# A fixed pipelined order for the last eight value projections, with the loads and the inversion at the delta rule's end rearranged

## The chip, the cores and the metric

The kernel runs on one core of a Trainium2 chip. The metric is the time of one execution on the device in microseconds (us). Five engines work side by side, each through its own instructions in order: PE (matmul), DVE (vector), ACT (scalar, also a DMA issuer), POOL (GpSimd) and SP (here only a DMA issuer). An instruction waits on semaphores for data of other engines and of DMA transfers; everything behind it on its engine waits too.

## The reference

One inference step of a two-layer encoder over 2048 prompt tokens and 32 sample tokens, 1024 wide, all in float32. Layer 1 is a gated delta rule of eight heads of 128, layer 2 is windowed attention. Cut to what the change touches:

```python
def causal_conv(x, buf, w):                      # four taps, then SiLU
    xp = jnp.concatenate([buf, x], axis=1)
    y = sum(xp[:, j:j + l] * w[j] for j in range(4))
    return jax.nn.silu(y), xp[:, -3:]

def delta_layer(x, conv_buf, s0, w_in, ...):
    proj = x @ w_in                              # q | k | v | z | a | b
    qkv, new_buf = causal_conv(proj[..., :3072], conv_buf, conv_w)
    q, k = l2norm(qkv[..., :1024]) * 128 ** -0.5, l2norm(qkv[..., 1024:2048])
    g, beta = -exp(a_log) * softplus(a + dt_bias), sigmoid(b)
    # blocks of positions: decay = exp(gcum_i - gcum_j); (I + lower) is inverted;
    # S = S * exp(gcum_last) + kdec^T v_new along the blocks
    o, s_new = gated_delta_rule(q, k, v, g, beta, s0)
    o = o * rsqrt(mean(o * o) + eps) * norm_w * silu(z)
    return layer_norm(ALPHA * x + o @ w_out, ln_g, ln_b), new_buf, s_new
```

The second layer projects queries and gates from the result, attends over the last two blocks of 64 and its own, and ends in a second output projection and layer norm.

## The kernel before

Every wide projection is split into three float32r products: weights and activations are each parted into a high part (a cast on ACT) and a low part (a subtraction on DVE or POOL), and `project` adds hi·hi, hi·lo and lo·hi in PSUM.

**Projection rows.** In `P1.qkv`, row i (0 to 23) is 128 columns of w_in: 0 to 7 are q heads, 8 to 15 k heads, 16 to 23 v heads. A row is five blocks of 416 tokens; a block is 24 matmuls (L77 to L79) into one of six PSUM banks, and ACT copies it to the row tile R (L258, two buffers). Weights come by SP into `w_raw` (L46, one buffer), ACT casts `w_hi` (L53), POOL subtracts `w_lo` (L54), two buffers each. Then the row's convolution: ACT writes the first tap (L198), DVE adds three more (L200, three instructions), ACT takes tanh (L203), DVE finishes SiLU (L204), SP stores 1 MB to `s_v` (L206; `s_k`, `s_q` for the other kinds). After each eighth row of q and k, `norms` runs a chain of small DVE operations on [128, 136].

**Work laid beside rows 16 to 23.** `decays` makes 34 decay matrices: a load of `gcum` into E (L231, ACT's queue, three buffers), an addition on DVE (L239), four exponentials on ACT (L243), a store to `s_E` (L244, ACT's queue). `split_out_weights` takes one piece of the output weights per row from row 7 on: fetch by SP (L1037) into the tile that tanh also uses, cast on ACT (L1038), subtraction on POOL (L1039), store `s_wo` by SP (L1040). In all of this the framework's scheduler sets each engine's order.

**Gate rows and the delta rule.** Rows 24 to 31 (`P1.z`) are the gate, of which three blocks each come ahead of the delta rule. `Delta.run` then walks 17 chunks (one of the sample, 16 of the prompt) through steps named in the table `ORDER`, which with a planner fixes PE, DVE and ACT; loads (`load`, L598 to L611) go by SP. Each chunk inverts a triangular matrix: the first `SPLIT` of 31 column steps on POOL (`early`, L661 and L663), the rest on DVE (`late`). In the last chunks a second generator, `O1.tiles`, the output projection with its norm (matmuls L1075 to L1077), is given out in small pieces as filler by `second.give`. Output weights come back by ACT's queue, slice by slice, at the calls of `side`; the tiles g (L1105), r (L1110) and the norm's tables (L1058, L1059) by SP. `first_end` finishes the sample chunk (transposes `otr<-ident,os` L848, gate L852). At the very end the last chunk's o is normalised (`OSC`, whose last step is L839) and transposed.

**Layer 2** begins by splitting the activations of its five blocks (L68, L69) under the first matmuls of `P2.gate`.

Of the kernel before, what the change touches and what calls it, by code (L numbers as in the profile page):

```python
# [18 lines left out]

D = 1024  # L20
NP = 2048
# [74 lines left out]
class P1:  # L96

    def __init__(self, tc, left, right, mid, I, O, T, G):  # L100
        self.nc, self.I, self.O, self.T, self.G = tc.nc, I, O, T, G
# [44 lines left out]
    def qkv(self):  # L146
# [31 lines left out]
        matrices = self.decays()  # L178
        wo = split_out_weights(nc, one, "th", I["a_w_out"], T["wo"])
        for i in range(24):  # L180
            kind, h = i // 8, i % 8
# [7 lines left out]
            if 7 <= i < 23:  # L189
                next(wo)  # L190
            if i >= 16:
                for _ in range(5 if i < 18 else 4):
                    next(matrices)
            nc.gpsimd.tensor_copy(self.convo[:, i, 0:3], R[:, NP:NP + 3])  # L194
            nc.gpsimd.tensor_copy(self.convo[:, i, 3:6], R[:, NT + 3:NT + 6])
            W = NT + 3
            y = big.tile([128, NT + 3], F32, tag="y", name="y")
            nc.scalar.activation(y[:], R[:, 0:W], AF.Copy, scale=self.convw[:, i, 0:1])  # L198
            for j in range(1, 4):
                nc.vector.scalar_tensor_tensor(out=y[:], in0=R[:, j:j + W], scalar=self.convw[:, i, j:j + 1], in1=y[:],  # L200
                                               op0=ALU.mult, op1=ALU.add)
            th = one.tile([128, NT + 3], F32, tag="th", name="th")
            nc.scalar.activation(th[:], y[:], AF.Tanh, scale=0.5)  # L203
            nc.vector.scalar_tensor_tensor(out=y[:], in0=th[:], scalar=1.0, in1=y[:], op0=ALU.add, op1=ALU.mult)  # L204
            dst = T["qkv"[kind]]
            nc.sync.dma_start(dst[0:NTT - 1, :, h, :].rearrange("t p k -> p t k"),  # L206
                              y[:, 0:NP].rearrange("p (t k) -> p t k", k=128))
            nc.scalar.dma_start(dst[NTT - 1, :, h, 0:NS], y[:, NP + 3:NP + 3 + NS])
            if kind == 2:
                continue  # L210
            nc.scalar.activation(th[:, 0:NP], y[:, 0:NP], AF.Square)
            nc.scalar.activation(th[:, NP:NT], y[:, NP + 3:NP + 3 + NS], AF.Square)
            nc.vector.transpose(R[:, 0:NT], th[:, 0:NT])
            nc.vector.tensor_reduce(out=parts[:, h, :], in_=R[:, 0:NT].rearrange("p (c j) -> p c j", j=32),
                                    axis=AX.X, op=ALU.add)
            if h == 7:
                norms(nc, G, parts, self.sel, kind, one, self.pt)
        nc.sync.dma_start(self.O["conv"][:, :, :], self.convo[:])

    def decays(self):  # L220
# [6 lines left out]
        def load(m):  # L227
# [3 lines left out]
            nc.scalar.dma_start(E[:, :, :n], T["gcum"][t, hs, :n].partition_broadcast(128))  # L231
            return E, t, n, hs

        ahead = load(0)
        for m in range(len(todo)):
# [8 lines left out]
            nc.scalar.dma_start(T["E"][t, :n, hs, :n], E[:n, :, :n])  # L244
# [15 lines left out]
    def z(self, blocks, pool, tags, ps, sub, w):  # L260

        nc = self.nc
        for h in range(8):
            self.fetched = fetch_weights(nc, self.wp, self.I["w_in"][25 + h]) if h < 7 else None
            self.next, self.sub = None, sub
            for b in blocks:
                p = ps()
                yield from project(nc, p[:, :TB], w, self.x[b])
                th = pool.tile([128, TB], F32, tag=tags[0], name="zth")
# [267 lines left out]
class Delta:  # L537
# [6 lines left out]
    SPLIT = 25  # L544
# [121 lines left out]
    def early(self, ch, j):  # L666
        cut = [self.SPLIT * i // 6 for i in range(7)]
        drain(self.chain(ch, self.nc.gpsimd, cut[j], cut[j + 1], "tm" if j == 0 else None))

    def late(self, ch, j):  # L670
        cut = [self.SPLIT + (31 - self.SPLIT) * i // 3 for i in range(4)]
# [231 lines left out]
    def run(self, chunks, S, gate, second, side, done):  # L903
# [4 lines left out]
        for c, ch in enumerate(chunks):  # L908
            ch.S, ch.last = (self.S if ch.pool is None else S), ch.pool is not None or c == last
        gate.plan(order, self.FIRST + 2, self.WHOLE)  # L910
        gate.begin()
        for i in range(self.FIRST, last + 4):
# [3 lines left out]
            for p, (name, off) in enumerate(order):  # L916
# [4 lines left out]
                elif 0 <= c <= last and self.wanted(chunks[c], name):  # L921
# [3 lines left out]
                    if c == last and name == "oa1":  # L925
# [3 lines left out]
                if i >= self.OPEN and p % (len(order) // 5) == 10:  # L929
# [4 lines left out]
    def first_end(self, c0, second, done):  # L934
        second.give(2.0)
# [3 lines left out]
        second.give(3.0)  # L939
# [4 lines left out]
        done(c0)  # L944

# [109 lines left out]
def ln_tables(nc, pool, g, b):  # L1055
    gt = pool.tile([128, D], F32, tag="ln_g", name="ln_g")
    bt = pool.tile([128, D], F32, tag="ln_b", name="ln_b")
    nc.sync.dma_start(gt[:], g.partition_broadcast(128))  # L1058
    nc.sync.dma_start(bt[:], b.partition_broadcast(128))  # L1059
# [30 lines left out]
class OutNorm:  # L1090


    def __init__(self, tc, es, name, side, I, pre, banks, kept):
# [4 lines left out]
        self.tabs = None  # L1098
        self.tables = lambda: ln_tables(nc, self.one, I[pre + "_ln_g"], I[pre + "_ln_b"])
# [3 lines left out]
    def fetch(self, src, n):  # L1103
        g = self.one.tile([128, KC, 128], F32, tag="g", name="g")
        self.nc.sync.dma_start(g[:, :, :n], src)  # L1105
# [52 lines left out]
class O1:  # L1158
# [13 lines left out]
    def turned(self, h, c0, row, n):  # L1172
# [3 lines left out]
        for q in range(2):  # L1176
# [4 lines left out]
            copy = nc.scalar.copy if q == 0 or c0 == 0 else nc.vector.tensor_copy  # L1181
# [5 lines left out]
    def tiles(self, tiles, ready, more):  # L1187
# [8 lines left out]
        for i, t in enumerate(tiles):  # L1196
# [5 lines left out]
            following = self.rows(*tiles[i + 1]) if i + 1 < len(tiles) else None  # L1202
            for j, out in enumerate(self.on.tile(got, r, t[2], True)):
# [15 lines left out]
class P2:  # L1219
# [26 lines left out]
    def load(self, b, res):  # L1246
# [8 lines left out]
        self.x[b] = split_acts(nc, res, b, raws, nc.gpsimd if b < 2 else nc.vector)  # L1255
# [105 lines left out]
class Attention:  # L1361
# [27 lines left out]
    def open_right(self, right):  # L1389
# [9 lines left out]
        self.tabs = ln_tables(self.nc, self.oone, I["b_ln_g"], I["b_ln_b"])  # L1399
# [444 lines left out]
```

## Time and profile before

| what | value |
|---|---|
| median of 3 runs | 2211.59 us (2209.03 to 2213.85) |
| profiled execution | 2210.17 us, its span 2208.4 us |
| PE busy | 2151.5 us, 97% of the span |
| DVE, ACT, POOL busy | 1373.8, 900.9, 825.7 us |
| mean granted clock of PE | 0.991 |
| DMA | 308.29 MB, 140 GB/s on average |

A busy row of PE counts matmuls whose ends are modelled. The views by stretch give busy time in each stretch and the granted clock of PE in it; the waits of PE name what ended each idle time. Value rows 16 to 23 run from about 398 to 589 us, the gate rows follow; the end of the delta rule lies from 1000 to 1170, layer 2 begins behind it.

### The profile page before, as it was taken

What the parts mean: (1) busy time and instruction counts of PE and PEld (TensorE: products, weight loads), DVE (VectorE), ACT (ScalarE), POOL (GpSimd) and SP (SyncE); (2) the same over time, 40 slices, a digit from 0 to 9 for tenths busy, and PEclk for the clock granted to TensorE, in tenths of its full rate; (3) what the DMA queues carried; (4) which work ended last, traced back from release to release, by engine and by line L of the source; (5) the groups of instructions that cost most, each with busy time, mean ns of one, the idle gap of its engine ahead of it and who ended that gap; (6) DMA issues with size and microseconds to landing.
All of it is one profiled execution on the core that took longest, in us unless ns stands there. A gap on an engine that the chain in (4) does not pass through costs nothing.

```text
span 2208.4 us, 36899 instructions
## 1 busy us (share of the span) xinstructions
PE 2151.5 (97%) x13690; PEld 1982.6 (90%) x13690; DVE 1373.8 (62%) x2701; ACT 900.9 (41%) x2274; POOL 825.7 (37%) x1201
## 2 busy tenths in 40 slices
PE   8999999999899999998999999999999999999998
PEld 6999999999899999998987887999999987778885
DVE  3676666664468588777867876125442236668775
ACT  4344344455522466665741212222112235544442
POOL 1422223211122377777720301046442124555564
PEclk9999999999999999999999999999999999999999
DMA  5222333356654544447735764365212287233321
GB/s 197 68 61 87 103 111 106 95 169 199 198 165 131 178 149 160 148 160 257 254 96 179 233 195 124 124 209 176 82 66 79 85 185 265 77 96 96 98 71 53
DMA packets 268116, 308.29 MB, mean 140 GB/s; under 512 B 79728, under 2 KB 198832, under 8 KB 267664
## 3 DMA queue, kind: packets, MB, share of 16 engines
q1 hardware_dynamic: 245696, 268.50, 39.1%
q10 hardware_dynamic: 22240, 37.42, 5.2%
q8 instruction: 108, 1.77, 0.3%
q14 instruction: 72, 0.59, 0.1%
HBM read 189.63 MB, written 116.60 MB: 139 GB/s over the span
## 4 chain that ended last, share of the span: by engine, by line
PE 65%; DMA 6%; DVE 3%; POOL 2%; ACT 1%; issue 1%; ACTq 0%; SPq 0%; DVEq 0%; POOLq 0%
PE ps L77 9%; PE ps L79 8%; PE ps L78 8%; PE po L1075 5%; PE po L1077 5%; PE po L1076 5%; PE ot L1567 4%; PE S L1546 2%; PE tr L1561 2%; DMA wo_parts<-in_a_w_out 1%; DMA E<-s_gcum 1%; PE g L627 1%; PE gq L754 1%; PE sp L769 1%; PE ks L769 1%; PE vp L769 1%
## 5 line engine op out<-in xcount | busy, mean ns | idle before, releaser
L77 PE MATMUL ps<-act_hi,w_hi 128*128 128x416 f32 x2000 | 708.5, 355 | 10.2 <-ACT R L258 6.1
L79 PE MATMUL ps<-act_hi,w_lo 128*128 128x416 f32 x2000 | 707.0, 354 | 3.3 <-POOL w_lo L301 1.8
L78 PE MATMUL ps<-act_lo,w_hi 128*128 128x416 f32 x2000 | 704.0, 352 | 2.5 <-DVE act_lo L69 2.5
L77 PEld LDWEIGHTS ps<-act_hi,w_hi 128*128 128x128 f32 x2000 | 377.8, 189 | 18.0 <-ACT R L258 7.1
L79 PEld LDWEIGHTS ps<-act_hi,w_lo 128*128 128x128 f32 x2000 | 377.4, 189 | 8.9 <-POOL w_lo L301 2.1
L78 PEld LDWEIGHTS ps<-act_lo,w_hi 128*128 128x128 f32 x2000 | 377.7, 189 | 8.4 <-DVE act_lo L69 3.9
L54 POOL TENSOR_TENSOR w_lo<-w_raw,w_hi 128x1024 fp32r<-128x1024 f32 x44 | 117.3, 2667 | 481.3 <-ACT w_hi L53 421.4
L200 DVE SCALAR_TENSOR_TENSOR y<-R,convw,y 128x2083 f32<-128x2083 f32 x72 | 181.8, 2526 | 41.3 <-POOL convo L194 22.5
L661 POOL TENSOR_TENSOR tm<-L,Tt 128x60 f32<-128x60 f32 (+19 forms) x375 | 130.4, 348 | 104.6 <-issue 40.2
L1554 POOL TENSOR_TENSOR P<-P,sm 128x384 f32<-128x384 f32 (+2 forms) x128 | 101.6, 816 | 169.2 <-DVE sm L1432 100.2
L663 POOL TENSOR_TENSOR Tt<-Tt,tm 128x60 f32<-128x60 f32 (+19 forms) x375 | 143.8, 384 | 29.4
L1428 ACT ACTIVATE P<-S,nm 128x192 f32<-128x192 f32 (+3 forms) x260 | 104.8, 418 | 90.5 <-DVE nm L1421 43.9
L258 ACT COPY R<-ps 128x416 f32<-128x416 f32 (+1 forms) x144 | 60.6, 444 | 131.0 <-PE ps L79 107.8
L1075 PE MATMUL po<-wo_hi,g_hi 128*128 128x512 f32 x256 | 104.3, 407 | 0.0
L1077 PE MATMUL po<-wo_hi,g_lo 128*128 128x512 f32 x256 | 100.8, 394 | 0.5 <-DVE g_lo L1118 0.5
L1076 PE MATMUL po<-wo_lo,g_hi 128*128 128x512 f32 x256 | 100.6, 393 | 0.0
L1272 POOL TENSOR_TENSOR rs<-rs,sin 128x416 f32<-128x416 f32 x50 | 70.6, 1413 | 78.1 <-DVE rs L1271 71.4
L1567 PE MATMUL ot<-pt,vd 128*128 128x256 f32 x372 | 97.9, 390 | 1.9 <-ACT pt L1563 1.4
L53 ACT CAST w_hi<-w_raw 128x1024 fp32r<-128x1024 f32 x48 | 50.4, 1049 | 112.6 <-PE ps L78 82.9
L1075 PE MATMUL po<-wo,g_hi 128*128 128x512 f32 x224 | 92.9, 415 | 0.0
L1357 DVE SCALAR_TENSOR_TENSOR za<-zs,za 128x416 f32<-128x416 f32 x40 | 33.3, 834 | 93.0 <-ACT za L1356 92.9
L1077 PE MATMUL po<-wo,g_lo 128*128 128x512 f32 x224 | 90.1, 402 | 0.0
(301 smaller groups left out, 4067.1 us busy)
## 6 DMA issues: line engine op xcount, KB each, us to landing
w_raw<-in_w_in SPq DMA_DIRECT2D x40, 512.0 KB
w_raw<-in_b_w_in SPq DMA_DIRECT2D x20, 512.0 KB
k<-s_k SPq DMA_DIRECT2D x17, 512.0 KB
E<-s_E SPq DMA_DIRECT2D x17, 512.0 KB
s_bz<-za SPq DMA_DIRECT2D x40, 208.0 KB
s_bq<-ra SPq DMA_DIRECT2D x40, 208.0 KB
s_q<-y SPq DMA_DIRECT2D x8, 1024.0 KB
s_wo<-wo_parts SPq DMA_DIRECT2D x16, 512.0 KB
```

The costliest lines, as they stand in the source:

```text
L54: sub.tensor_tensor(out=lo[:], in0=raw[:], in1=hi[:], op=ALU.subtract)
L77: nc.tensor.matmul(ps, hi[:, k, :], xh[:, k, :], start=(k == 0), stop=False)
L78: nc.tensor.matmul(ps, hi[:, k, :], xl[:, k, :], start=False, stop=False)
L79: nc.tensor.matmul(ps, lo[:, k, :], xh[:, k, :], start=False, stop=(k == KC - 1))
L200: nc.vector.scalar_tensor_tensor(out=y[:], in0=R[:, j:j + W], scalar=self.convw[:, i, j:j + 1], in1=y[:], op0=ALU.mult, op1=ALU.add)
L661: P.tensor_tensor(out=tm[:n, i0 - k:, :w], in0=L[:n, i0:, j:j + 1].to_broadcast(sh), in1=Tt[:n, j:j + 1, :w].to_broadcast(sh), op=ALU.mult)
L663: P.tensor_tensor(out=Tt[:n, i0:, :w], in0=Tt[:n, i0:, :w], in1=tm[:n, i0 - k:, :w], op=ALU.subtract)
L1075: nc.tensor.matmul(ps[:n], ghi[:, k, :n], w[0][:, k, cs], start=a, stop=False)
L1076: nc.tensor.matmul(ps[:n], ghi[:, k, :n], w[1][:, k, cs], start=False, stop=False)
L1077: nc.tensor.matmul(ps[:n], glo[:, k, :n], w[0][:, k, cs], start=False, stop=z)
L1428: nc.scalar.activation(P[u], src, AF.Exp, bias=nm[:, u:u + 1], scale=1.0, accum_out=sm[:, u:u + 1])
L1567: nc.tensor.matmul(ot[:, p], self.vd[:, kc0 + j, p, :], pt[:, 2 * j:2 * j + 2, :], start=(j == 0), stop=(j == nj - 1))
```

## The change

It has three parts. **(A)** Rows 0 to 15 stay as they were (their convolutions up to 14). For rows 16 to 23, `ordered` writes the order of PE, DVE, ACT and SP by hand: in row i, `conv` of row i − 1 is dealt out in steps between the five blocks, one decay matrix is made ahead of each block of rows 17 to 23, and one output weight piece per row follows the convolution's store. The loads and stores of E, and the short store of each row, go by SP's queue instead of ACT's. The tail of row 23's convolution is dealt out between the first 13 steps of the gate rows, which for that take two tiles of the old pool. **(B)** In the delta rule's last chunks (behind number 11, `OPEN`) `SPLIT` is 23 instead of 25; the loads of g, r and the norm's tables in that part go by ACT's queue (`self.queue`, until the first tile of the rest), the output weights in four calls of `side` per chunk instead of five; `first_end` is called behind `OSC` of the last chunk and not behind `oa1`, and gives 5.5 us of filler in one piece ahead of the sample chunk's transposes and 1.5 behind. **(C)** Gate block 0 of layer 2's second slab moves ahead into the filler's last part; block 2's activation subtraction goes from DVE to POOL; the last short tile's copies go to DVE.

```diff
-        for i in range(24):
+        for i in range(self.FREE + 1):            # FREE = 15
...
+            if i < self.FREE:
+                drain(self.conv(i, R, parts))
+        with self.tc.manual_schedule(engines={ET.PE, ET.DVE, ET.Activation, ET.SP}):
+            self.ordered(R, parts, wo)
...
+    def ordered(self, R, parts, wo):
+        nc, I = self.nc, self.I
+        w = split_weights(nc, self.wp, I["w_in"][self.FREE + 1], nc.gpsimd)
+        matrices = None
+        for i in range(self.FREE + 1, 24):
+            c = self.conv(i - 1, R, parts)
+            nxt = self.row(i)
+            raw = fetch_weights(nc, self.wp, I["w_in"][i + 1])
+            next(c)
+            for b in range(NB):
+                if matrices:
+                    next(matrices, None)
+                for _ in range((2, 2, 1, 1, 0)[b]):
+                    next(c, None)
+                if b == 3:
+                    next(wo)
+                self.block(nxt, w, b)
+                if b == 0:
+                    following = split_fetched(nc, self.wp, raw, nc.gpsimd)
+            drain(c)
+            R, w = nxt, following
+            if i == self.FREE + 1:
+                matrices = self.decays()
+                next(matrices)
+        self.room = self.one, ("parts", "gtmp")
+        self.tail = self.conv(23, R, parts)
+        next(self.tail)
+        self.w24 = w
...
-            nc.scalar.dma_start(E[:, :, :n], T["gcum"][t, hs, :n].partition_broadcast(128))
+            nc.sync.dma_start(E[:, :, :n], T["gcum"][t, hs, :n].partition_broadcast(128))
-            nc.scalar.dma_start(T["E"][t, :n, hs, :n], E[:n, :, :n])
+            nc.sync.dma_start(T["E"][t, :n, hs, :n], E[:n, :, :n])
...
+    with tc.manual_schedule(engines={ET.PE, ET.DVE}):
+        for a, b in ((2, 5), (2, 4), (1, 4)):
+            for _ in range(a):
+                next(p1.tail)
+            for _ in range(b):
+                next(z)
+        drain(p1.tail)
...
-    SPLIT = 25
+    SPLIT = 25, 23
+            ch.split = self.SPLIT[c > self.OPEN]
...
-                    if c == last and name == "oa1":
+                    if c == last and name == "OSC":
                         self.first_end(chunks[0], second, done)
-                if i >= self.OPEN and p % (len(order) // 5) == 10:
+                if i >= self.OPEN and p % (len(order) // 4) == 10:
...
     def first_end(self, c0, second, done):
-        second.give(2.0)
...
-        second.give(3.0)
+        second.give(5.5)
...
+        second.give(1.5)
...
+        self.tabs, self.queue = None, nc.scalar
-        self.nc.sync.dma_start(g[:, :, :n], src)
+        self.queue.dma_start(g[:, :, :n], src)
-        self.nc.sync.dma_start(r[:n], src)
+        self.queue.dma_start(r[:n], src)
...
-        self.x[b] = split_acts(nc, res, b, raws, nc.gpsimd if b < 2 else nc.vector)
+        self.x[b] = split_acts(nc, res, b, raws, nc.gpsimd if b < 3 else nc.vector)
...
+            if i == 2:
+                yield from p2[0].gate(1, (0,), p2[0].ps)
```

The order of SP in the value rows, one row of before (E's transfers were on ACT's queue):

```order
L206 DMA s_v<-y 128x16x128
L1037 DMA wo_parts<-in_a_w_out 128x512
L46 DMA w_raw<-in_w_in 128x1024
L1040 DMA s_wo<-wo_parts 128x2x512
L206 DMA s_v<-y 128x16x128
```

and the same place after, from the store of one row's third matrix on (L271 and L285 are E's load and store, L216 and L218 the stores of v, L1080 and L1083 the fetch and store of the output weights, L47 the next weights):

```order
L271 DMA E<-s_gcum 128x512
L285 DMA s_E<-E 128x512
L216 DMA s_v<-y 128x16x128
L218 DMA s_v<-y 128x32
L1080 DMA wo_parts<-in_a_w_out 128x512
L1083 DMA s_wo<-wo_parts 128x2x512
L271 DMA E<-s_gcum 128x512
L285 DMA s_E<-E 128x512
L47 DMA w_raw<-in_w_in 128x1024
L271 DMA E<-s_gcum 128x512
```

The first load of the next row's matrices now stands behind the store of the output weights, and the store of v behind that of a matrix.

DVE at the end of the key norms, before (L398 to L405 are the norms, L200 and L204 row 16's and 17's convolution, L239 a matrix):

```order
L239 TENSOR_TENSOR E<-E,nm 128x512
L398 SCALAR_TENSOR_TENSOR n_lt<-n_ly,n_lt 128x136
L399 TENSOR_TENSOR n_ly<-n_lt 128x136
L400 TENSOR_SCALAR n_lx<-n_ly 128x136
L402 SCALAR_TENSOR_TENSOR n_lx<-n_lx,n_ly 128x136 x6
L403 TENSOR_SCALAR n_lx<-n_lx 128x136
L200 SCALAR_TENSOR_TENSOR y<-R,convw,y 128x2083
L404 TENSOR_TENSOR n_lx<-n_lx,n_lt 128x136
L200 SCALAR_TENSOR_TENSOR y<-R,convw,y 128x2083
```

and after (L442 to L447 the norms, L207 and L213 the convolution, now of row 16, L280 a matrix):

```order
L442 TENSOR_SCALAR n_lx<-n_ly 128x136
L444 SCALAR_TENSOR_TENSOR n_lx<-n_lx,n_ly 128x136 x6
L445 TENSOR_SCALAR n_lx<-n_lx 128x136
L446 TENSOR_TENSOR n_lx<-n_lx,n_lt 128x136
L447 TENSOR_TENSOR t_ngc<-t_ngc,n_lx 128x136
L280 TENSOR_TENSOR E<-E,nm 32x4x32
L207 SCALAR_TENSOR_TENSOR y<-R,convw,y 128x2083 x2
L280 TENSOR_TENSOR E<-E,nm 32x4x32
L207 SCALAR_TENSOR_TENSOR y<-R,convw,y 128x2083
L280 TENSOR_TENSOR E<-E,nm 128x512
L213 SCALAR_TENSOR_TENSOR y<-th,y 128x2083
```

The norms are one piece now, and row 16's convolution begins behind them.

DVE at the end of the last chunk, before (otr_11916 and otr_11923 are the sample chunk's transposed o, otr_11962 the last chunk's; L817 updates the state, L839 is the end of OSC):

```order
L1083 SCALAR_TENSOR_TENSOR r<-r,po 128x512
L1135 BN_STATS st<-r 128x6
L852 TENSOR_TENSOR z<-otr_11916,z 128x4x32
L852 TENSOR_TENSOR z<-otr_11923,z 128x4x32
L817 SCALAR_TENSOR_TENSOR Sp<-Sp,t_egl,sp_11868 128x128 x4
L830 SCALAR_TENSOR_TENSOR Xo<-Xo,t_eq 128x8
```

and after, from the end of OSC (L881) on:

```order
L881 TENSOR_TENSOR o<-o,ro_y 128x1024
L1161 TENSOR_TENSOR g_lo<-g,g_hi 128x1024
L1126 SCALAR_TENSOR_TENSOR r<-r,po 128x512
L1178 BN_STATS st<-r 128x6
L894 TENSOR_TENSOR z<-otr_11960,z 128x4x32
L1126 SCALAR_TENSOR_TENSOR r<-r,po 128x512
```

The sample chunk's gate (otr_11960) stood ahead of the last chunk's state and OSC, and now stands behind them.

More of the change, by code (lines that the diff above doesn't have):

```diff
@@ L188, in qkv @@
                     self.block(R, w, b)
-            if 7 <= i < 23:
+            if 7 <= i < self.FREE:
                 next(wo)
[L191 to L205, printed above, removed]
@@ L1180, in turned @@
                 nc.tensor.transpose(tr[:, j, :n], h[:n, k * 128:k * 128 + 128], self.G["ident"][:n, :n])
-            copy = nc.scalar.copy if q == 0 or c0 == 0 else nc.vector.tensor_copy
+            copy = nc.scalar.copy if n == 128 and (q == 0 or c0 == 0) else nc.vector.tensor_copy
             copy(hT[:, q * 4:q * 4 + 4, :n], tr[:, :, :n])
@@ L1607, in program @@
     next(ahead)
-    w = p1.first_gate(nc.gpsimd)
-    z = p1.z((0, 1, 2), zp, ("zth", "z"), p1.ps, nc.gpsimd, w)
-    with tc.manual_schedule(engines={mybir.EngineType.PE, mybir.EngineType.DVE}):
-        for _ in range(28):
+    with tc.manual_schedule(engines={ET.PE, ET.DVE}):
+        for _ in range(15):
             next(z)
@@ L1661, in program @@
     o1[0].bank = p2[0].ps
-    with tc.manual_schedule(engines={ET.PE, ET.DVE}):
-        second.rest()
-    left.close()
-    p2 = p2[0]
     with tc.manual_schedule(engines={ET.PE}):
+        with tc.manual_schedule(engines={ET.DVE}):
+            second.rest()
+        left.close()
+        p2 = p2[0]
         p2.open_left(left)
-        drain(p2.gate(1, (0, 1), p2.ps))
+        drain(p2.gate(1, (1,), p2.ps))
     for b in (2, 3, 4):
```

75 lines of the change are left out of this document (49 added, 26 removed).

## The prediction

> **What bounds the kernel now.** I read the page first, then PE's waits, then busy time by stretches of 40 us, and then the rows around each wait.
>
> The page's rows of busy time, as engine, busy us, share of the span, instructions:
>
> ```profile
> span 2208.4 us, 36899 instructions
> PE 2151.5 (97%) x13690; PEld 1982.6 (90%) x13690; DVE 1373.8 (62%) x2701; ACT 900.9 (41%) x2274; POOL 825.7 (37%) x1201
> ```
>
> PE bounds it: only 2208.4 − 2151.5 = 57 us of PE's time are idle. No edit here removes a matmul from PE, so a gain is idle time taken away plus work no longer done at the low clock, and any new idle time of PE is a loss. The change reaches PE's idle time in three places. Place A is the value projections; the stretches (us, then busy time of PE, PEld, DVE, ACT, POOL, the granted clock, DMA share, GB/s) and PE's waits from 398 to 645:
>
> ```profile
> 480.00:520.00 40.00, 40.00 (x214) 39.73 (x213) 22.18 (x17) 20.64 (x48) 5.01 (x8) 1.00 0.66 199
> 520.00:560.00 40.00, 38.44 (x205) 37.84 (x203) 16.13 (x12) 20.47 (x49) 7.05 (x7) 1.00 0.66 201
> 560.00:600.00 40.00, 35.41 (x169) 34.30 (x170) 21.64 (x16) 22.69 (x52) 6.59 (x9) 0.91 0.63 203
> 600.00:640.00 40.00, 35.91 (x192) 34.31 (x191) 19.15 (x15) 15.00 (x22) 8.56 (x5) 0.96 0.61 168
> ...
> PE ps L77 <- ACT R L258: 6.1, 2, 3.2
> PE ps L77 <- ACT w_hi L309: 2.3, 1, 2.3
> PE ps L79 <- POOL w_lo L301: 1.8, 1, 1.8
> ```
>
> PE idles 6.1 + 2.3 + 1.8 = 10.2 us here, all after 556. The clock of 0.91 and 0.96 in the two stretches after idle time means about (0.09 + 0.04) × 40 = 5 us of work lost at the low clock. A perfect order is worth 15 us at place A. PE ran full until about 556 although ACT and DVE were behind, because its six PSUM banks and two weight sets let it run ahead.
>
> Place B is the end of the delta rule: stretches, PE's waits (1015 to 1170), one wait of DVE.
>
> ```profile
> 1000.00:1040.00 40.00, 37.54 (x462) 35.92 (x460) 34.75 (x92) 28.66 (x95) 32.28 (x90) 1.00 0.81 289
> 1040.00:1080.00 40.00, 34.74 (x354) 33.93 (x354) 27.61 (x68) 24.23 (x80) 25.69 (x76) 0.91 0.75 267
> 1160.00:1200.00 40.00, 35.74 (x161) 29.66 (x162) 27.93 (x78) 6.44 (x8) 2.99 (x2) 0.91 0.61 187
> ...
> PE otr L848 <- DVE o L839: 5.7, 1, 5.7
> PE g L627 <- DMA k<-s_k: 4.2, 1, 4.2
> PE y1p L697 <- DVE tcp L678: 2.6, 2, 1.6
> PE vtr L741 <- DMA v<-s_v: 2.0, 1, 2.0
> ...
> DVE tm L661 <- POOL Tt L663: 6.3, 3, 2.4
> ```
>
> Each 0.91 is 0.09 × 40 = 3.6 us lost at the low clock.
>
> **Place A, part by part.** Here the change writes one order for PE, DVE, ACT and SP. What decides is the loop from one value row to the next. From 495 to 526 before shows every link of it; the columns are start, duration, engine, line, operation, and the idle time with its releaser:
>
> ```profile
> 495.51 0.38 SPq L206 DMA_DIRECT2D s_v<-y  x1
> 500.67 2.39 POOL L54 TENSOR_TENSOR w_lo<-w_raw,w_hi 128x1024 fp32r<-128x1024 f32 x1 [11.14 <-ACT w_hi L53]
> 502.88 0.62 ACT L1038 CAST wo_parts<-wo_parts 128x512 fp32r<-128x512 f32 x1 [1.83 <-DMA wo_parts<-in_a_w_out]
> 504.16 0.33 ACTq L231 DMA_DIRECT2D E<-s_gcum  x1
> 505.35 1.26 ACT L243 ACTIVATE E<-E,t_ngc 128x128 f32<-128x128 f32 x4
> 505.50 0.38 SPq L1040 DMA_DIRECT2D s_wo<-wo_parts  x1
> 507.93 0.69 DVE L239 TENSOR_TENSOR E<-E,nm 128x512 f32<-128x512 f32 x1 [3.60 <-DMA E<-s_gcum]
> 511.44 4.80 DVE L200 SCALAR_TENSOR_TENSOR y<-R,convw,y 128x2083 f32<-128x2083 f32 x2
> 517.99 1.95 ACT L203 ACTIVATE th<-y 128x2083 f32<-128x2083 f32 x1 [3.15 <-DVE E L239]
> 521.68 2.32 DVE L204 SCALAR_TENSOR_TENSOR y<-th,y 128x2083 f32<-128x2083 f32 x1
> 524.03 0.38 SPq L206 DMA_DIRECT2D s_v<-y  x1
> ```
>
> Before, the loop takes 524.03 − 495.51 = 28.5 us. In the new order it is, link by link: s_v issued until the output weight behind it has landed, 502.88 − 495.51 = 7.4; its cast and subtraction until s_wo is issued, 505.50 − 502.88 = 2.6. Only then does SP issue the next row's first load of a decay matrix, where ACT used to issue it beside this: 0.4. From that issue to its use 507.93 − 504.16 = 3.8, and about 1.5 more since the 0.5 MB of s_wo now stand ahead in the same queue (an estimate: half of what those 7.4 us hold beside the 3.8 of a lone transfer, which is 1 MB's share). Then DVE in its fixed order: addition 0.7, three convolution steps with an addition between, 1.5 × 4.80 + 0.7 = 7.9; tanh 1.95; last step 2.3. SP next owes the store of the fourth matrix, so one more addition and four exponentials, 0.7 + 1.3 + 0.4 = 2.4, before the next s_v. Sum: 7.4 + 2.6 + 0.4 + 5.3 + 0.7 + 7.9 + 1.95 + 2.3 + 2.4 = 31 us. As the three or four gaps that ACT's own issues made there go, I take **30 us a row**, 28 to 32 for its bounds. PE needs 22.5 a row (five blocks of 24 matmuls, full in 480 to 520 with 214 in 40 us).
>
> What waits behind this on PE: the weights of row i+1 are cast on ACT only behind row i's first exponentials and first copy, so PE's start follows the loop once about a row of lead is used up. The loop also starts later: all small operations of the key norms stand on DVE ahead of the first value row's convolution, where before they lay between its steps. The rows of before: the reduction that the norms need, two of the norms' operations, and PE's first matmul of the first gate row:
>
> ```profile
> 419.58 2.32 DVE L214 TENSOR_REDUCE parts<-R 128x65 f32<-128x2080 f32 x1
> 435.52 0.30 DVE L443 SCALAR_TENSOR_TENSOR n_t<-n_x,n_y 128x136 f32<-128x136 f32 x1
> 435.86 0.30 DVE L445 TENSOR_TENSOR n_t<-n_t,n_y 128x136 f32<-128x136 f32 x1
> 589.22 0.62 PE L77 MATMUL ps<-act_hi,w_hi 128*128 128x416 f32 x1 [2.98 <-ACT R L258]
> ```
>
> 35 such operations at 435.86 − 435.52 = 0.34 are 12 us, from about 423 (419.58 + 2.32, and the norms' matmuls) to 435. Row 18's weights are then ready at 435 + 0.7 (addition) + 1.3 (exponentials) + about 1.5 (copy and cast on ACT) + 2.4 (w_lo on POOL), near 440, and those of the first gate row, number 24, six loops later at 440 + 180 = 620. Before, PE began that row at 589.2. So +31, less what before still lost behind that point (waits of 2.3 and 1.8, the 1.6 of clock 0.96 and about half of the 3.6 of 0.91: 7.5), plus 1.7 for the low clock behind a new wait of 7 us: **+25**, from +13 (28 us a row) to +37 (32). If PE stayed full all the way it would be −15. Row 23's convolution moves between the first 13 steps of the gate rows; its four large steps on DVE (about 10 us) lie beside 13 quarters of a block, 15 us of matmuls, and cost PE nothing; were they not covered, it would be one wait of about 3 us for a bank. The Trainium skill (DMA: Bandwidth & Descriptors, Issuing engines are not separate DMA queues) says that issuing on several engines saves only the sequencer's time to start a DMA; by that sentence alone, moving the matrices from ACT to SP is free, and place A would come out at its gain of 15. The trace's rows speak against free: the row of 505.50 shows SP held until the subtraction is done, and the load would now stand behind it.
>
> **Place B.** First, a burst of 2.5 MB (g, the two norm tables, two residual tiles) goes from SP to ACT's queue, about 90 us later; the loads of the output weights go from five to four per chunk.
>
> ```profile
> 1017.04 2.20 SPq L1105 DMA_DIRECT2D g<-s_g  x1
> 1036.53 0.32 SPq L598 DMA_DIRECT2D k<-s_k  x1
> ```
>
> The queues are full behind it (DMA share 0.81), k lands 8 us after its issue, and PE waits 2.0 + 4.2. That goes, and the 3.6 at the low clock: −9 (if other loads keep the queue full, −3). On ACT five issues now stand between the last chunk's copies; by the rows above one is 0.32 to 2.2 us, two or three of them on PE's path: +1.5 (0 to +4). Second, the split: two of 25 inversion steps of the last five chunks go from POOL to DVE. PE's 2.6 us for tcp hang on DVE's 6.3 us for POOL. POOL saves 2 × (0.348 + 0.384) = 1.5 us a chunk by the page's means of L661 and L663; what DVE adds I bound by the same 1.5 and by nothing:
>
> ```profile
> L661 POOL TENSOR_TENSOR tm<-L,Tt 128x60 f32<-128x60 f32 (+19 forms) x375 | 130.4, 348 | 104.6 <-issue 40.2
> L663 POOL TENSOR_TENSOR Tt<-Tt,tm 128x60 f32<-128x60 f32 (+19 forms) x375 | 143.8, 384 | 29.4
> ```
>
> Net −1.5 (0 to −2.6). Third, the sample chunk's end is placed behind the last chunk's normalised output instead of ahead of it:
>
> ```profile
> 1158.37 0.54 DVE L852 TENSOR_TENSOR z<-otr,z 128x128 f32<-128x128 f32 x2 [1.66 <-PE otr L848]
> 1164.26 1.08 PE L848 MATMUL otr<-ident,o 128*128 128x128 f32 x4 [5.68 <-DVE o L839]
> ```
>
> DVE idled 1.66 for os, and o was there only at 1164.2. Without that wait, the gate steps for os (0.54 × 2) and one residual addition with its statistics (1.4) ahead of it, o is there near 1159 to 1160. PE has six more matmuls and four transposes (about 2 us) to do before it asks for o, so from 1158.6, where it began to wait, it goes on to about 1160.6: −5.7 − 3.6 + 0.5 of DVE work moved behind, about **−8.5** (−5 to −9). Place B: −9 + 1.5 − 1.5 − 8.5 = **−17.5**, from −8 to −22.
>
> **Place C**, the start of layer 2's projection, 1360 to 1395:
>
> ```profile
> PE ps L78 <- DVE act_lo L69: 2.5, 4, 1.3
> PE ps L77 <- ACT act_hi L68: 1.8, 2, 1.0
> ```
>
> Half a pair of blocks is moved ahead as cover and block 2's subtraction goes to POOL: of 4.3 us and about 1.7 at the low clock I take −3 (−6 if all goes, +2 if POOL's 2.4 us for a subtraction, the row of 500.67, take the place of DVE's).
>
> **Sum.** +25 − 17.5 − 3 = +4.5. The profiled execution took 2210.2 (span 2208.4), so it would take 2214.7; the median of the runs lies 1.4 above it, which makes **2216**. About 0.2% (4.4 us) is what a measurement of this kernel can tell from no change, so the forecast stands at that edge, on the slow side. Its own range, with a loop of 29 to 31 us and B from −22 to −12, is 2205 to 2222.
>
> The low clock in the sum is the trace's 0.91; the Trainium skill (TensorE: Matmul & The Clock Gate, What's actually happening) gives 3.4 us at half rate behind an idle window. By that each of about five new waits of 7 us costs 1.7; I count only the last, since the earlier rows have 7 us of slack against the loop. The trace's stretch of 560 to 600 shows low clock behind waits of only 3 us.
>
> **The rivals.** (1) *PE stays full, or nearly, at A*: the loop comes out at 26 us or less because ACT no longer stops for issues and landings (the tanh row has 3.15 idle ahead of it, and ACT is busy half of the time). At 25 and below A is −15 to −5 and the kernel ends at 2211.6 − 15 − 17.5 − 3 = 2176 to 2186; at 26 A is +1 and it ends at 2192. Against it: s_v, output weight, s_wo and the next load stand in one line on SP, 7.4 + 2.6 + 0.4 + 5.3 = 16 us by themselves, and the DVE and ACT steps that follow are another 15. (2) *One queue makes the loop longer still*, and from about 30 us a row on the kernel is slower by more than 4.4: at 32 us it ends at 2211.6 + 37 − 17.5 − 3 = 2229. For it: the DMA share is 0.66 in this stage with two queues at work, and now one carries all. (3) *B does not pay*: the 2.5 MB and the output weights meet other loads later, so that −9 is −3, and ACT's five issues cost 4; B is then −9 and the kernel ends at 2211.6 + 25 − 9 − 3 = 2225. For it: the 16 output-weight loads still run beside the chunks' loads. (4) *What binds at A is something that the order doesn't touch*, and the rest is hidden: 2212 ± 3.
>
> **How the numbers follow.** Forecast: 0.35, of it 0.05 faster, 0.14 within 4.4 us and 0.16 slower. Rival 1: 0.26, all faster, half of it below 2184. Rival 2: 0.19 and rival 3: 0.15, all slower. Rival 4: 0.05, the same. Faster 0.05 + 0.26 = 0.31; same 0.14 + 0.05 = 0.19; slower 0.16 + 0.19 + 0.15 = 0.50. The range 2184 to 2234 leaves out the fuller half of rival 1 (0.13) and a loop over 33 us (0.05).
>
> **What would show it.** In the profile after: s_v stores of rows 18 to 22 spaced 28 to 32 us; PE waits of 5 to 9 us for w_hi or w_lo at the start of each of rows 20 to 24; the output-weight store followed at once on SP by a load of E, whose addition ends DVE's longest idle time. At B no wait of PE for k near 1040, none for o at the last chunk, a clock of 1.00 there. I am wrong if the s_v stores come every 23 to 26 us and PE shows no wait in 440 to 640, or if the waits at B stay with other names.

## The result: slower by 1.5%, and where the time went

The changed kernel takes 2243.5 us (median of 4 runs, 2242.5 to 2246.7) against 2210.7 of before (now also a median of 4): a ratio of 1.0149, interval 1.0132 to 1.0167, or +32.8 us. The forecast was 2216, its range ended at 2234. The direction was right, the size was not. The page of after:

```profile
span 2242.2 us, 36907 instructions
PE 2158.0 (96%) x13690; PEld 1988.5 (89%) x13690; DVE 1387.3 (62%) x2718; ACT 899.4 (40%) x2273; POOL 833.9 (37%) x1185
```

PE runs the same 13690 matmuls and is busy 6.5 us longer, at a mean granted clock of 0.985 where before had 0.991; the rest of the loss is idle time. The same matmul, found in both traces by its place among those of its kind, shows where the lag arises:

| matmul of | before, us | after, us | lag | arisen since the row above |
|---|---|---|---|---|
| first value row | 398.22 | 398.28 | 0.1 | |
| first gate row's start | 589.22 | 630.35 | 41.1 | +41.1, value rows |
| gate rows, middle | 699.97 | 750.67 | 50.7 | +9.6, behind the value rows |
| delta rule, chunk near 1020 | 1019.99 | 1070.68 | 50.7 | 0 |
| behind the loads of 1017 | 1059.96 | 1102.88 | 42.9 | −7.8, loads and split |
| output projection, 1130 | 1130.04 | 1172.15 | 42.1 | −0.8 |
| behind the sample chunk's end | 1199.99 | 1233.84 | 33.9 | −8.3, sample chunk's end |
| layer 2, behind its first blocks | 1410.04 | 1440.35 | 30.3 | −3.5, place C |
| attention | 1900.15 | 1934.03 | 33.9 | +3.6 |

Places B and C gave −16.9 and −3.5, where −17.5 and −3 were forecast. Place A cost 50.7 instead of 25 (the first two rows of losses together), and 3.6 more came up in the attention stage. The +9.6 is itself a sum: +3.7 for a second wait at the first gate row, −5.5 where before had waits of its own just behind 589 (the lag is 39.3 at 615 of before's time), and +11.4 at the first inversion.

**Place A in the trace of after.** The stretches, columns as in the prediction, and PE's waits from 440 to 700:

```profile
480.00:520.00 40.00, 34.18 (x167) 33.12 (x166) 17.73 (x12) 16.44 (x39) 6.33 (x6) 0.91 0.54 167
520.00:560.00 40.00, 33.96 (x169) 32.90 (x168) 14.65 (x9) 18.46 (x39) 7.93 (x9) 0.91 0.51 157
560.00:600.00 40.00, 28.99 (x134) 27.00 (x132) 20.49 (x13) 16.48 (x36) 8.06 (x7) 0.87 0.55 167
600.00:640.00 40.00, 30.92 (x141) 29.69 (x142) 19.83 (x12) 16.87 (x36) 8.75 (x8) 0.83 0.49 151
...
PE ps L80 <- POOL w_lo L55: 20.7, 6, 3.6
PE ps L78 <- ACT w_hi L54: 16.2, 6, 3.7
PE g L669 <- DMA k<-s_k: 9.5, 1, 9.5
PE ps L78 <- ACT R L299: 0.4, 1, 0.4
```

At each of six row starts (rows 19 to 24, where 20 to 24 were forecast) PE waits twice, for the high part and, at its third matmul, for the low part of its weights: 16.2 + 20.7 = 36.9 us, 6.2 a row, as forecast (5 to 9). The DMA share fell from 0.66 to about 0.52: the transfers are not the limit, they stand in line. One turn of the loop, SP, then ACT, POOL and DVE, sorted by engine:

```profile
547.28 0.43 SPq L216 DMA_DIRECT2D s_v<-y  x1
547.75 2.27 SPq L218 DMA_DIRECT2D s_v<-y  x1
550.06 1.23 SPq L1080 DMA_DIRECT2D wo_parts<-in_a_w_out  x1
556.18 0.37 SPq L1083 DMA_DIRECT2D s_wo<-wo_parts  x1
556.97 1.23 SPq L271 DMA_DIRECT2D E<-s_gcum  x1
...
554.16 0.62 ACT L1081 CAST wo_parts<-wo_parts 128x512 fp32r<-128x512 f32 x1 [7.27 <-DMA wo_parts<-in_a_w_out]
562.97 1.28 ACT L284 ACTIVATE E<-E,t_ngc 128x128 f32<-128x128 f32 x4 [4.09 <-DVE E L280]
564.54 1.04 ACT L54 CAST w_hi<-w_raw 128x1024 fp32r<-128x1024 f32 x1
565.66 4.20 POOL L55 TENSOR_TENSOR w_lo<-w_raw,w_hi 128x1024 fp32r<-128x1024 f32 x1 [8.57 <-ACT w_hi L54]
...
562.25 0.69 DVE L280 TENSOR_TENSOR E<-E,nm 128x512 f32<-128x512 f32 x1 [13.36 <-DMA s_E<-E]
562.86 4.81 DVE L207 SCALAR_TENSOR_TENSOR y<-R,convw,y 128x2083 f32<-128x2083 f32 x2
567.58 2.83 DVE L280 TENSOR_TENSOR E<-E,nm 128x512 f32<-128x512 f32 x1
570.33 2.38 DVE L207 SCALAR_TENSOR_TENSOR y<-R,convw,y 128x2083 f32<-128x2083 f32 x1
574.76 2.33 DVE L213 SCALAR_TENSOR_TENSOR y<-th,y 128x2083 f32<-128x2083 f32 x1 [1.46 <-ACT th L211]
```

The loop runs as the prediction wrote it: store of v (547.28), weights landed and cast (554.16), their store (556.18), and only then the next row's first load (556.97), whose addition (562.25) ends DVE's longest idle time of the turn, 13.36. (The row names the last of several things that this addition waits for, E's store; its wait for the load of 556.97 ends at 562.11.) Up to here 15.0 us, forecast 15.7. The convolution steps then take 562.86 to 572.71, 9.85 instead of 7.9, since the addition between them takes 2.83 us and not 0.69. Tanh, last step and the matrix ahead of the store are as forecast, and the next store of v comes at 579.46: 32.2 us. From the second store of v to the sixth, 484.15 to 611.33, the mean is 31.8.

### The profile page after: what moved, and what is told of

The parts are those of the page before. It is cut to its first block, busy times and chain, and to the rows that moved or that the text cites. A ratio compares the mean times of both kernels' runs of the same rounds, so it can differ in the third digit from the quotient of the medians.

```text
span 2242.2 us, 36907 instructions
## 1 busy us (share of the span) xinstructions
PE 2158.0 (96%) x13690; PEld 1988.5 (89%) x13690; DVE 1387.3 (62%) x2718; ACT 899.4 (40%) x2273; POOL 833.9 (37%) x1185
## 4 chain that ended last, share of the span: by engine, by line
PE 63%; DVE 3%; DMA 2%; ACT 1%; issue 1%; SPq 0%; POOL 0%; DVEq 0%; ACTq 0%; POOLq 0%
PE ps L78 8%; PE ps L80 8%; PE ps L79 8%; PE po L1118 5%; PE po L1120 5%; PE po L1119 5%; PE ot L1611 4%; PE S L1590 2%; PE tr L1605 2%; PE g L669 1%; PE ks L811 1%; PE gq L796 1%; PE sp L811 1%; PE vp L811 1%; PE op L841 1%; PE op L835 1%
## 5 line engine op out<-in xcount | busy, mean ns | idle before, releaser
L80 PE MATMUL ps<-act_hi,w_lo 128*128 128x416 f32 x2000 | 713.3, 357 | 21.8 <-POOL w_lo L55 21.8
L78 PEld LDWEIGHTS ps<-act_hi,w_hi 128*128 128x128 f32 x2000 | 381.8, 191 | 30.7 <-ACT w_hi L54 22.3
L55 POOL TENSOR_TENSOR w_lo<-w_raw,w_hi 128x1024 fp32r<-128x1024 f32 x44 | 130.4, 2964 | 471.0 <-ACT w_hi L54 435.2
L207 DVE SCALAR_TENSOR_TENSOR y<-R,convw,y 128x2083 f32<-128x2083 f32 x72 | 181.7, 2524 | 43.2 <-ACT y L204 29.5
L703 POOL TENSOR_TENSOR tm<-L,Tt 128x60 f32<-128x60 f32 (+19 forms) x365 | 124.5, 341 | 99.3 <-issue 40.2
L705 POOL TENSOR_TENSOR Tt<-Tt,tm 128x60 f32<-128x60 f32 (+19 forms) x365 | 143.7, 394 | 28.6
L280 DVE TENSOR_TENSOR E<-E,nm 128x512 f32<-128x512 f32 (+1 forms) x34 | 37.6, 1105 | 95.2 <-DMA s_E<-E 66.3
L1401 DVE SCALAR_TENSOR_TENSOR za<-zs,za 128x416 f32<-128x416 f32 x40 | 32.2, 808 | 94.9 <-ACT za L1400 94.8
```

The lines of the kernel that those rows point to most:

```text
L55: sub.tensor_tensor(out=lo[:], in0=raw[:], in1=hi[:], op=ALU.subtract)
L78: nc.tensor.matmul(ps, hi[:, k, :], xh[:, k, :], start=(k == 0), stop=False)
L80: nc.tensor.matmul(ps, lo[:, k, :], xh[:, k, :], start=False, stop=(k == KC - 1))
L703: P.tensor_tensor(out=tm[:n, i0 - k:, :w], in0=L[:n, i0:, j:j + 1].to_broadcast(sh), in1=Tt[:n, j:j + 1, :w].to_broadcast(sh), op=ALU.mult)
L705: P.tensor_tensor(out=Tt[:n, i0:, :w], in0=Tt[:n, i0:, :w], in1=tm[:n, i0 - k:, :w], op=ALU.subtract)
```

## The experiments

All are compared with before (2207.8 to 2210.8 us beside them). Those without a ratio are one run each. "Lag" is that of the same matmul against before, as in the table.

**The value rows undone.** The first kernel is after, with `P1` and the start of the gate rows put back to before.

> The rows, matrices and gate rows are as before; the delta rule's end and layer 2's start are as after. Theory (the loss is all in the value rows and at their end, B and C gained as the two traces show, -16.9 and -3.5): 2210.7 - 20.4 = 2190, no wait of PE for k or o in the delta rule. Rival (B's gain only exists because A delays everything by 50 us, so that other transfers meet there): 2200 or more. If the 3.6 us that after lost in the attention stage belong to B or C, 2194.

It took 2185.5 us, 4.5 less than expected, ratio 0.9898 (0.9881 to 0.9914). B and C alone gain; the rival that B lives from A's delay falls. The lag goes from −2.0 at 1020 to −20.5 at 1200 and −26.1 at 1410, so B gave −18.5 and C −5.6; at 1900 it is −26.7, so the attention's 3.6 did not come up here.

**The output weights taken out of the loop.**

```diff
-                if b == 3:
-                    next(wo)
...
+            if i < 8:   # in the first rows, low parts left out
+                k, c = 4 + i // 2, slice(512 * (i % 2), 512 * (i % 2) + 512)
+                for a in range(2):
+                    nc.sync.dma_start(T["wo"][a, k, :, c], I["a_w_out"][k][:, c])
```

> After, but the eight pieces of the output weights that were split inside rows 16 to 23 are copied unsplit from memory to memory in rows 0 to 7; their low parts are left out. Theory (a loop on SP's order: store of v, fetch, cast, subtraction, store of the weights, then the next row's first load): that link of 7 to 8 us goes, the stores of v come every 24 to 25 us instead of 32, time near 2195 to 2200. Rival (one queue carries too many bytes): 0.75 of about 5 MB a row go, 32 becomes 27 us, time near 2215. Rival (DVE and POOL hold each other up): stays at 31 to 32, 2240.

2199.8 us. The stores of v come at 485.8, 511.4, 537.1, 562.8, 588.8, 614.1: 25.7 us apart, so 6.1 us a row went of the 7 to 8 expected. The time fits, although the added copies delay the first rows by 8 us (lag 8.1 at 398): from there to 700 the lag grows by only 0.7, so the value rows did better than the total says. DVE and POOL still collided here (one addition of 2.83 to 2.89 in each row behind the first).

**The low part of the weights on DVE.**

```diff
-                    following = split_fetched(nc, self.wp, raw, nc.gpsimd)
+                    following = split_fetched(nc, self.wp, raw, nc.vector)
```

> After, with the low part of the weights of rows 17 to 24 subtracted on DVE in its fixed order instead of POOL. Theory (the second matrix addition of a row takes 2.83 instead of 0.69 us because POOL's subtraction runs at the same time, which in turn takes 4.2 instead of 2.4): the addition is back at 0.7, the subtraction takes 1.2 on DVE, the loop is 0.9 us shorter, time near 2237. Rival (the addition is slow for its own data): it stays 2.8 and the loop grows by 1.2, time near 2250.

2233.6 us. The two rows, E's additions of after and of this kernel between 440 and 640 (durations in ns, least, median, most):

```profile
L280 DVE TENSOR_TENSOR E<-E,nm x32: 673/692/2831, 440.6 to 637.3; 128x512 f32<-128x512 f32 x31, 32x128 f32<-32x128 f32 x1
...
L280 DVE TENSOR_TENSOR E<-E,nm x33: 273/685/694, 441.5 to 636.0; 128x512 f32<-128x512 f32 x32, 32x128 f32<-32x128 f32 x1
...
L55 DVE TENSOR_TENSOR w_lo<-w_raw,w_hi x7: 1218/1218/1219, 440.3 to 625.5; 128x1024 fp32r<-128x1024 f32 x7
```

No addition is longer than 0.69 any more, and the stores of v are 30.7 apart (512.5 to 604.7 in three rows), although DVE does 1.22 us more in each. Without either the loop would be near 29.5 (30.7 − 1.2, an estimate). So the 2.1 us are the collision with POOL, not the addition's own data.

**More gate steps ahead of the first inversion** (25 in place of 15 in the loop over `next(z)`).

> After, with 25 gate steps instead of 15 ahead of the first inversion's Gram product. Theory (PE reaches that product before row 23's store and the loads behind it on SP are through): PE's wait of 9.5 us for k goes, with the low clock 11 us in all, time near 2232. Rival (the loads of the first chunks follow one another and the wait only moves to v or q): 2240 or more. The value rows stay at 32 us in both.

2225.8 us. PE's waits from 640 to 700 are empty, the lag between 589 and 700 goes from 39.6 to 38.4, where after went from 41.1 to 50.7; the rival's wait for v or q didn't come. That is 10.8 of the 17.7 gained in this run. About 3.3 more lie in the attention stage (lag +0.3 there and not +3.6), 1.5 in the value rows, and the rest at places B and C (−1.7 and −1.0); none of these was touched, so differences of this size between single runs mean little.

**A second order on SP**: the output weights' fetch ahead of the store of v, the next row's first load ahead of it too, the weights' store last, and 25 gate steps. The cut shows the row's loop alone.

```diff
-                for _ in range((2, 2, 1, 1, 0)[b]):
+                for _ in range(((2, 2, 1, 1, 0) if i == self.FREE + 1 else (2, 2, 1, 0, 1))[b]):
                     next(c, None)
-                if b == 3:
+                if b >= 3:            # first call fetches and splits, second stores
                     next(wo)
```

> After, with a different fixed order on SP in rows 17 to 23 and 25 gate steps first: the output weights are fetched ahead of the store of v, then comes the next row's first matrix load, then the store of v, and the store of the output weights last. Theory (the loop is SP's order, so the next row's load no longer hangs on the store of v and the weights): the stores of v come at PE's own 22.5 us, PE has no wait of over 1 us in 440 to 640, time near 2176 (-12 at the value rows, -17, -3.5, no wait for k). Rival (one queue with 5 MB a row, which at 22.5 us would be 222 GB/s where before moved about 203): 25 us or more a row, time 2188 or more. Rival (DVE and POOL's collision is what matters): above 2200.

2207.2 us, ratio 0.9982 (0.9970 to 0.9994). This expectation missed: rows of 28.6 us (457.6 to 600.5 in five), not 22.5. By its time and its rows alone this run would leave the rival of the bytes standing; the last run below takes it away. The trace names another link of the same line:

```profile
514.42 0.43 SPq L217 DMA_DIRECT2D s_v<-y  x1
514.89 2.17 SPq L219 DMA_DIRECT2D s_v<-y  x1
517.11 1.23 SPq L1087 DMA_DIRECT2D s_wo<-wo_parts  x1
518.38 0.68 SPq L47 DMA_DIRECT2D w_raw<-in_w_in  x1
519.10 1.14 SPq L273 DMA_DIRECT2D E<-s_gcum  x1
...
524.25 1.04 ACT L54 CAST w_hi<-w_raw 128x1024 fp32r<-128x1024 f32 x1 [6.15 <-DMA w_raw<-in_w_in]
```

The next weights and the second matrix now stand behind both stores in the queue, and ACT holds still for the weights until 5.9 us after their issue.

**One store moved**: as after, with the output weights' store behind the next row's first load.

> After, with one instruction moved: the store of the output weights is issued behind the next row's first matrix load and not ahead of it. Theory: only the 2.0 us of cast and subtraction and the 1.5 of the transfer ahead leave the way of that load; ACT's cast still waits 7 us for the weights, with the row's last copies and the next row's first tap behind it, so the loop falls from 32 to about 29, time near 2227. If the load of E alone made the loop: below 27 and 2215 or less. If its place doesn't matter: 32 and 2243.

2220.0 us, stores of v 28.2 to 29.7 apart (480.3 to 595.3 in four rows: 28.8). 29 was expected; the time is 7 lower than expected. The place of this one instruction is worth 3.0 us a row (31.8 to 28.8).

**The value rows alone.**

> Before, with the new order of the value rows and the start of the gate rows alone. Theory (the parts add): 2210.7 + 39.3 + 11.4 = 2261, up to 2265 with the attention's 3.6. Rival (the end of the delta rule depends on what comes before): its waits differ from before's 4.2 for k and 5.7 for o.

2264.2 us, inside the 2261 to 2265 expected. PE's waits at the delta rule's end for k are 4.4, like before's 4.2, and a wait for o stays. Place by place the halves agree within about 2 us (B −18.5 without A and −16.9 with it, C −5.6 and −3.5). Added up, this run and the first give +54.6 − 25.3 = +29.3 where after has +32.8; the 3.5 left over were not followed.

**The three parts of B alone**: the split; the loads; the sample chunk's end.

> Before, with 23 of 31 inversion steps on POOL in the last five chunks alone. Theory (prediction): PE's waits for tcp shrink from 2.6 to about 1, -1.5 us in 1060 to 1130. Rival (DVE takes back in the steps what it no longer waits): 0.

> Before, with only the loads at the delta rule's end spread: g, r and the norm's tables by ACT's queue later, output weights four times a chunk. Theory: PE's waits of 4.2 for k and 2.0 for v near 1040 and the low clock behind them go, -8.4 as after's trace has it, and ACT's issues cost PE less than 1.5 near 1110. Rival (the wait comes back behind the moved loads): 0 to -3.

> Before, with only the sample chunk's end behind the last chunk's normalised output. Theory: PE's wait of 5.7 for o and the low clock behind it go, -8.3. Rival (the sample chunk's transposes or the residual tiles are late in their place): a wait of 2 us or more elsewhere in 1150 to 1200, -4 or less.

2202.1, 2203.7 and 2203.2 us (one run each; before 2209.6, and 2207.8 for the last two). PE's waits from 1015 to 1170 in the three:

```profile
PE otr L848 <- DVE o L839: 5.4, 1, 5.4
PE g L627 <- DMA k<-s_k: 2.0, 1, 2.0
PE y1p L697 <- DVE tcp L678: 1.2, 3, 0.4
PE vtr L741 <- DMA v<-s_v: 1.2, 1, 1.2
...
PE otr L848 <- DVE o L839: 5.5, 1, 5.5
PE y1p L697 <- DVE tcp L678: 2.2, 2, 1.5
PE g L627 <- DMA k<-s_k: 2.1, 2, 1.7
...
PE g L627 <- DMA k<-s_k: 4.2, 1, 4.2
PE y1p L697 <- DVE tcp L678: 2.6, 2, 1.5
PE vtr L741 <- DMA v<-s_v: 2.0, 1, 2.0
```

The sample chunk's end alone gives −8.3 between 1130 and 1200 (forecast −8.5): its wait for o is gone from the third group. The loads alone give −6.4 between 1020 and 1060 and nothing more up to 1130; so ACT's issues, at 1101 to 1106 in that run, show no cost, where +1.5 was forecast. The split alone gives −5.2 between 1020 and 1060 and −3.1 from there to 1170, far over the −1.5 expected; with both in place (after) it is −7.8 and −0.8. They are two ways to much the same 6 to 8 us: either halves PE's wait for k (4.2 to about 2). That the split should act on a load was in neither account. The order of SP tells how, before first, then the split alone:

```profile
1034.76 0.38 SPq L601 DMA_DIRECT2D E<-s_E  x1
1036.53 0.32 SPq L598 DMA_DIRECT2D k<-s_k  x1
...
1033.78 0.38 SPq L598 DMA_DIRECT2D k<-s_k  x1
1036.02 0.32 SPq L601 DMA_DIRECT2D E<-s_E  x1
```

With the split, k's load stands ahead of E's instead of behind it and goes out 2.75 us earlier. The kernel writes no order for SP here, so the split gained there by a swap that nobody planned; a run with the swap alone is missing.

**A third order**: the second with the next weights fetched from inside the row before, the output weights' cast behind the fourth matrix and their store in the next row, and w_lo on DVE.

```diff
+                if b == 0 and i > self.FREE + 1:
+                    next(wo)                       # store of the row before
...
+                if b >= 3:
+                    next(wo)                       # b 3: fetch, b 4: cast, subtract
...
-                    following = split_fetched(nc, self.wp, raw, nc.gpsimd)
+                    following = split_fetched(nc, self.wp, raw, nc.vector)
+                if b == 1 and i < 23:
+                    raw = fetch_weights(nc, self.wp, I["w_in"][i + 2])
```

> The kernel of the second order, with three more links taken out of the row's loop: the next weights are fetched behind the first blocks of the row before and not behind the stores, the output weights are cast behind the fourth matrix's exponentials and stored in the next row, and w_lo is subtracted on DVE. Theory (a loop of fixed orders on SP, ACT and DVE; PE needs 22.5): 23 to 24.5 us a row, no wait of PE over 2 us in 440 to 620, time 2176 to 2186. Rival (the bytes of one queue): the loop stays at 28, time 2205. Rival (another link of the order takes over): 25 to 27, time near 2190 to 2200, with a wait named in the trace.

2170.5 us (2169.6 to 2172.3), ratio 0.9814 (0.9797 to 0.9830): faster than both kernels, and than the first experiment. Its stretches and two stores of v:

```profile
480.00:520.00 40.00, 40.00 (x214) 39.73 (x213) 26.39 (x19) 23.53 (x53) 3.14 (x7) 1.00 0.72 222
520.00:560.00 40.00, 40.00 (x214) 39.73 (x213) 28.68 (x19) 24.73 (x52) 4.82 (x10) 1.00 0.74 227
560.00:600.00 40.00, 40.00 (x215) 39.78 (x214) 19.80 (x12) 20.83 (x42) 9.57 (x8) 1.00 0.65 193
600.00:640.00 40.00, 40.00 (x225) 39.20 (x224) 21.84 (x26) 10.77 (x18) 5.68 (x3) 1.00 0.64 177
...
498.28 0.43 SPq L217 DMA_DIRECT2D s_v<-y  x1
520.28 0.43 SPq L217 DMA_DIRECT2D s_v<-y  x1
```

PE is full at the full clock through all value rows, the stores from 453.5 to 564.5 come at PE's pace (21.8 to 22.5 us), and one queue moves 222 to 227 GB/s, where before's two moved 199 to 201. The lag is −16.2 at 700, all of the 15 that place A had to give and one more. The same work in the same queue costs 50.7 or gives 16.2, by order, by the engine of one subtraction and by ten more gate steps (of the difference, the 11.4 at the first inversion). What each of the new links gave was not taken apart.

## Why the prediction was right or wrong, step by step

**The loop: right in its mechanism, 2 us short in its size, six times.** This is the first step that failed, the term "30 us a row". The prediction's sum of links was 31 us, from which it took 1 for "gaps that ACT's own issues made". Measured 31.8 to 32.2: the links up to the first addition came 0.7 shorter than summed, one addition 2.1 longer, and the deduction of 1 had no row of its own. x2 and x6 show that the line on SP is the loop (25.7 and 28.8 us with one link out or moved), x11 that the bytes of one queue are not. Six loops of 2 us make 12 of A's excess. The chain's start makes 3: row 18's low part was ready at 438.46 + 4.53 = 443.0 and not at 440, for POOL's subtraction took 4.53 and not 2.4, and the links summed to 440.9. With the 25 forecast that is 40, against the 39.3 measured behind the first gate row, ahead of the first inversion (x4: 38.4). Up to here the time would still lie in the range: 2216 + 14 = 2230.

**What no term had: the start of the inversions.** The second step that failed is that row 23's convolution, moved between the gate steps, would "cost PE nothing", or one wait of 3 us for a bank. The prediction looked at PE and DVE and not at what stands behind that row's store on SP. Before first, then after:

```profile
621.07 0.37 SPq L206 DMA_DIRECT2D s_v<-y  x1
621.54 1.87 SPq L598 DMA_DIRECT2D k<-s_k  x1
...
670.21 0.37 SPq L216 DMA_DIRECT2D s_v<-y  x1
670.63 3.41 SPq L218 DMA_DIRECT2D s_v<-y  x1
676.23 1.10 SPq L640 DMA_DIRECT2D k<-s_k  x2
...
681.03 0.64 PE L669 MATMUL g<-k 128*32 128x32 f32 x8 [9.50 <-DMA k<-s_k]
```

The first inversions' loads stand on SP behind that store. It came 40 us after the gate rows' start (32 in before), and k's load 6.0 us behind it (0.5 in before), 3.41 of them in the issue of the short store. PE had 28 gate steps to do and then waited 9.5 us, 11.4 with the low clock behind it. x4 shows it: 25 steps of cover instead of 15, and the wait is gone. With this term the sum would have been 2216 + 14 + 11 = 2241, and the rest of the 2243.5 is within what the attention stage added.

**The low clock.** The prediction counted one new stretch of it, 1.7 us behind a wait of 7 and without a row for that figure, and held the others to be covered by slack. Behind the wait of 9.5 us it was 11.4 − 9.5 = 1.9. The granted clock of 0.91, 0.91, 0.87 and 0.83 in the stretches from 480 to 640 is more than 1.7 a row start (0.09 × 40 = 3.6 us in the first), but it lies inside rows that wait for the loop anyway; the loop's own links account for the 39, so that step agrees with the trace.

**Place B: right, −16.9 for −17.5.** The wait for o went (−8.3, forecast −8.5), the loads and the split gave −8.6 (forecast −9 + 1.5 − 1.5 = −9). The parts are not what they were thought to be, though: the split alone is worth −8.3 and not −1.5, the loads alone −6.4 and not −9, ACT's issues cost nothing, and loads and split overlap. That the sum of the first two came out is in part luck. **Place C: right**, −3.5 for −3; without A it was −5.6.

**Sums.** Three figures of the prediction do not follow from its terms, and none of them moves the forecast: B's bounds by its parts are −4 to −21 and not −8 to −22, its own range ends at 2211.6 + 31 − 12 − 3 = 2228 and not at 2222, and rival 2's time is 2228 and not 2229.

**The rivals.** "The loop is longer still" came true in its number, 32 us, but its reason, one queue with too much to carry, falls with x11's 227 GB/s. The others fall too: the loop was not below 28, B paid, and the time is not 2212. The rule of the Trainium skill (DMA: Bandwidth & Descriptors, Issuing engines are not separate DMA queues), by which issuing DMAs on several engines saves only the time to start them, agrees with x11, where one queue carried all at 222 to 227 GB/s. What cost was SP's fixed order of waiting instructions, which the rule doesn't speak of.

**Open.** In the attention stage PE waits 3.3 us for w_hi near 1830 in after and for nothing of that kind in before. The runs have it between 0 (x1, lag −26.1 to −26.7) and 3.6, with the same instructions there. What sets it wasn't tried.

## What to carry to other kernels

A fixed order over several engines puts all their waits into one loop: write down that loop link by link from the trace, in the new order, and compare it with the bound engine's time per turn before fixing it. Every DMA issue that waits for something (here the output weights' store) should stand behind the loads that must not come late, and loads should stand a turn ahead, not behind this turn's stores. When a stage's last store moves, look for the first load behind it in the same queue and for who waits for that.

## What the runs showed of the hardware

The addition on DVE and the subtraction on POOL do not share, they take turns. In the rows above DVE's second convolution step ends at 562.86 + 4.81 = 567.67; POOL's subtraction, begun at 565.66, ends at 569.86, which is 2.2 after that step, about its own time (2.39 in before); the addition, begun at 567.58, ends at 570.41, 0.55 after POOL. So POOL waited for DVE and then DVE for POOL, 1.8 and 2.1 us; in all six rows behind the first one addition took 2.83. The Trainium skill (SBUF — State Buffer, SBUF: two separate sides) says this: a pair of ports is held by one of the two for a whole instruction, for a DVE operation with two inputs in SBUF against a GpSimd operation that reads SBUF. The trace agrees, and x3 removes both sides of it at once. In before the scheduler's order had them apart, with luck: the additions there were 0.69, at most 1.06, and the subtractions 2.39, at most 2.86.

The second thing is the price of an issue behind a large transfer on the same queue: 2.27 us for the 16 KB behind the store of v, 3.41 at 670.63, where a lone one takes 0.3 to 0.4. The same 16 KB took 0.39 in before, issued on ACT's queue at the same moment as the large store on SP's.
